# The other experts' rows added to x by accumulating gathers, and the last expert's second product made in two column halves

## The chip, the core and the metric

The kernel runs on one core of a Trainium2 chip. The core has a matrix engine (TensorE, PE in the rows), a vector engine (VectorE, DVE), a scalar engine (ScalarE, ACT), a general engine (GpSimd, POOL) and an engine that mostly issues transfers (SyncE, SP). Each engine works through its own instructions in order and they meet at semaphores; sixteen DMA engines move data between DRAM and the on-chip memory SBUF. The metric is device time in microseconds, the median of several executions. All arithmetic is float32.

## What is computed

The program is a two-layer network on 512 tokens of width 1024. The change touches only the end of the second layer, a mixture of eight experts of which each token takes two, and the normalisation behind it:

```python
def swiglu(x, w1, w3, w2):
    return (jax.nn.silu(x @ w1) * (x @ w3)) @ w2

def moe_ffn(x, router_w, router_b, w1, w3, w2):
    logits = (x @ router_w).astype(jnp.float32) + router_b
    top_val, top_idx = lax.top_k(logits, TOP_K)
    weights = jax.nn.softmax(top_val, axis=-1)
    combine = jnp.sum(jax.nn.one_hot(top_idx, N_EXPERTS, dtype=jnp.float32) * weights[..., None], axis=-2)
    y = jnp.zeros_like(x)
    for e in range(N_EXPERTS):
        y = y + combine[..., e:e + 1].astype(x.dtype) * swiglu(x, w1[e], w3[e], w2[e])
    return y

...
        x = layer_norm(DN_ALPHA * x + y, ln_g[layer, 1], ln_b[layer, 1])
    return x
```

Here D_MODEL is 1024, D_FF_EXPERT 1408, N_EXPERTS 8, TOP_K 2.

## The kernel before

Tokens are sorted to experts: each expert has 128 slots, and 32 more for an overflow, which a branch skips where an expert has no more than 128 tokens (`further`, line 1453). `moe` (line 1765) loops over the experts. For each it gathers its tokens' rows, turns them so that the contraction lies on the partitions, and makes the two products with w1 and w3 in three column chunks (`up`, line 1410; 512, 512 and 384 columns). `turn` (line 1469) turns the gated result, and `down` (line 1493) makes the product with w2. Every float32 product is made of three matmuls: a weight block is loaded by SP into one of nine raw buffers (`moe_raw`), ACT casts it to a rounded part (`whi`, line 1164), and DVE subtracts to get the rest (`wlo`, line 1165). A raw buffer is free again after the branch in which the overflow slots would use it. While `ring` is set four more buffers serve.

For experts 0 to 6 the product y of 128 slots by 1024 columns is copied from PSUM by ACT (columns 0 to 511) and DVE (512 to 1023) and written by POOL to a DRAM array Y (lines 1532 to 1534); the overflow slots follow one step later (`down_more`, line 1538). Each token then knows two rows of Y (`slot`, made in `slots`, line 1676); a token's place in the last expert points at a zero row. In the last expert `ask_rows` (line 1707) gathers these rows, a block of 128 tokens and one of its two choices at a time, into the former ring buffers, and `take_rows` (line 1714) scales them on ACT by the token's weight and adds them to x on POOL:

```python
self.nc.scalar.mul(rows, rows, self.wt[:, tb, j:j + 1])
for half in range(2):
    xs = self.x[tb][half]
    self.nc.gpsimd.tensor_add(xs, xs, rows[:, half * 512:(half + 1) * 512])
```

The last expert's own product does not go through Y. `last` (line 1739) splits it, spreads it over the tokens by one-hot matmuls (`ohl`, lines 1755 to 1758), adds it to x on DVE (line 1760) with the token's weight, takes statistics (`stats`, line 248), normalises (`layer_norm`, lines 255 to 267) and stores.

The instructions of each engine are put in order by a scheduler from the written order and from priorities: `high_priority` and `hot` pull what they enclose forward, and `chain` keeps the weight loads in order. `weights` (line 1656) turns the router's two best scores into weights per token and expert (`cw`).

## Time and profile before

| | |
|---|---|
| device time, median of 3 runs | 2099.56 us (2098.76 to 2100.62) |
| the profiled execution: time / span of its instructions | 2099.76 us / 2098.0 us |
| PE busy | 2005.5 us, 96% |
| DVE busy | 1365.4 us, 65% |
| ACT busy | 916.3 us, 44% |
| POOL busy | 155.1 us, 7% |
| mean granted TensorE clock | 0.988 |

The span runs from the first instruction to the last; times in rows count from its start. The second layer's experts take about the last quarter of it. In a row of an engine's timeline stand the start, the duration, the engine, the line of the code and the operation, what it writes and from what, its shape and how many were merged; in brackets stand the time for which the engine was idle before it and what it waited for. Matmul durations overlap, so the rate of matmuls is read from their starts.

### The profile page before, as it was taken

The page shows a single profiled execution, that of the slowest core. Times are in us where ns is not written, and L with a number is a line of the kernel's source. Part 1 is how long each engine was busy: PE and PEld are TensorE (multiplying, and loading weights), DVE is VectorE, ACT ScalarE, POOL GpSimd, SP SyncE. Part 2 cuts the span into 40 slices and gives each one's busy share as a digit, 9 for nine tenths or more (in the row PEclk, how much of TensorE's full clock was granted, in tenths as well). Part 3 has the DMA queues.
Part 4 walks back from the last instruction along what each step waited for, and adds up shares of the span by engine and source line. Part 5 has one row for each costly group of instructions (what it writes and reads, how often), then busy time and mean ns, then how long its engine had stood idle before and what let it go on. Part 6 is the DMA issues. An engine that isn't in the chain of part 4 may idle for free. (4 is left out here: it accounts for less than half of the span.)

```text
span 2098.0 us, 31138 instructions
## 1 busy us (share of the span) xinstructions
PE 2005.5 (96%) x11240; PEld 1561.3 (74%) x11240; DVE 1365.4 (65%) x2732; ACT 916.3 (44%) x1561; POOL 155.1 (7%) x211
## 2 busy tenths in 40 slices
PE   8999999999999999999999999999989999999984
PEld 7767778778888888888767678778877766677663
DVE  5776779844563333236676779843668877788778
ACT  3464543333232222113454543332326666677663
POOL 1020200000000000000001200000010000000043
PEclk9999999999999999999999999999999999999997
DMA  5231213243243334333221213223538988898872
GB/s 166 71 78 37 58 51 91 81 126 101 91 151 95 101 94 133 91 100 115 77 57 44 70 36 90 84 64 101 196 112 313 350 296 304 284 351 304 291 284 78
DMA packets 274976, 294.56 MB, mean 140 GB/s; under 512 B 23852, under 2 KB 203416, under 8 KB 274808
## 3 DMA queue, kind: packets, MB, share of 16 engines
q1 hardware_dynamic: 267736, 273.90, 40.3%
q0 software_dynamic: 7072, 18.49, 2.8%
q8 instruction: 97, 1.59, 0.3%
q14 instruction: 71, 0.58, 0.1%
HBM read 276.74 MB, written 15.60 MB: 139 GB/s over the span
## 5 line engine op out<-in xcount | busy, mean ns | idle before, releaser
L99 DVE TENSOR_TENSOR wlo<-wraw,whi 128x1024 fp32r<-128x1024 f32 (+1 forms) x218 | 265.4, 1218 | 361.3 <-ACT whi L98 357.4
L98 ACT CAST whi<-wraw 128x1024 fp32r<-128x1024 f32 (+1 forms) x218 | 228.1, 1047 | 622.1 <-PE ps_mm L112 375.7
L113 PE MATMUL ps_mm<-xh,wlo 128*128 128x512 f32 (+1 forms) x1288 | 492.8, 383 | 3.1 <-DVE wlo L99 3.1
L111 PE MATMUL ps_mm<-xh,whi 128*128 128x512 f32 (+1 forms) x1288 | 494.6, 385 | 0.5 <-ACT whi L98 0.4
L112 PE MATMUL ps_mm<-xl,whi 128*128 128x512 f32 (+1 forms) x1288 | 492.4, 383 | 0.2 <-DVE xl L233 0.2
L113 PEld LDWEIGHTS ps_mm<-xh,wlo 128*128 128x128 f32 x1288 | 243.5, 189 | 49.0 <-DVE wlo L99 3.4
L112 PEld LDWEIGHTS ps_mm<-xl,whi 128*128 128x128 f32 x1288 | 243.5, 189 | 45.4 <-issue 2.1
L111 PEld LDWEIGHTS ps_mm<-xh,whi 128*128 128x128 f32 x1288 | 243.2, 189 | 45.3 <-issue 1.9
L1165 DVE TENSOR_TENSOR wlo<-mwraw,whi 128x1024 fp32r<-128x1024 f32 (+1 forms) x98 | 124.1, 1281 | 18.0 <-ACT whi L1164 16.6
L1164 ACT CAST whi<-mwraw 128x1024 fp32r<-128x1024 f32 (+1 forms) x98 | 95.9, 1006 | 16.4 <-PE ps_t L1515 10.2
L472 ACT COPY bt_pt<-ps_t 128x512 f32<-128x512 f32 (+2 forms) x80 | 41.8, 523 | 87.2 <-PE ps_t L467 86.7
L1165 DVE TENSOR_TENSOR mwlo<-mwraw,mwhi 128x1024 fp32r<-128x1024 f32 (+1 forms) x62 | 71.8, 1174 | 6.6 <-ACT mwhi L1164 6.2
L451 ACT ACTIVATE bt_pt<-ps_s,mx 128x256 f32<-128x256 f32 (+3 forms) x128 | 61.9, 488 | 17.5 <-DVE mx L445 14.2
L260 POOL TENSOR_TENSOR rs<-rs,mhalf 128x1 f32<-128x1 f32 x16 | 13.8, 861 | 721.0 <-DVE rs L259 721.0
L442 DVE TENSOR_REDUCE mx<-ps_s 128x2 f32<-128x512 f32 (+3 forms) x80 | 48.5, 607 | 22.5 <-PE ps_s L406 21.8
L1164 ACT CAST mwhi<-mwraw 128x1024 fp32r<-128x1024 f32 (+1 forms) x62 | 61.0, 999 | 3.1 <-DMA mwraw<-in_exp_w_dram 2.0
L1126 DVE TENSOR_TENSOR bt_pt<-bt_pt,ps_mm 128x512 f32<-128x512 f32 x22 | 15.1, 688 | 69.9 <-PE ps_mm L113 62.5
L622 DVE MAX8 m<-bt_pt 128x8 f32<-128x256 f32 (+2 forms) x96 | 53.7, 560 | 2.6
L467 PE MATMUL ps_t<-ident,bt_pt 128*128 128x128 f32 x272 | 45.1, 281 | 8.5 <-DVE bt_pt L461 5.9
L1165 DVE TENSOR_TENSOR wlo<-ring,whi 128x1024 fp32r<-128x1024 f32 (+1 forms) x45 | 51.4, 1158 | 2.5 <-ACT whi L1164 2.4
L623 DVE MATCH_REPLACE8 bt_pt<-m,bt_pt 128x256 f32<-128x256 f32 (+2 forms) x96 | 52.1, 543 | 0.0
L111 PE MATMUL ps_mm<-bt_o,whi 128*128 128x512 f32 x128 | 50.9, 397 | 0.4 <-ACT bt_o L524 0.4
(710 smaller groups left out, 4116.4 us busy)
## 6 DMA issues: line engine op xcount, KB each, us to landing
mwraw<-in_exp_w_dram SPq DMA_DIRECT2D x124, 512.0 KB
wraw<-in_w_in_dram SPq DMA_DIRECT2D x106, 512.0 KB
wraw<-in_ffn_w_dram SPq DMA_DIRECT2D x66, 512.0 KB
ring<-in_exp_w_dram SPq DMA_DIRECT2D x60, 512.0 KB
wraw<-in_exp_w_dram SPq DMA_DIRECT2D x32, 512.0 KB
mwraw<-in_exp_w_dram SPq DMA_DIRECT2D x36, 384.0 KB
wraw<-in_w_branch_dram SPq DMA_DIRECT2D x20, 512.0 KB
wraw<-in_w_out_dram SPq DMA_DIRECT2D x16, 512.0 KB
```

The lines of the kernel that those rows point to most:

```text
L98: nc.scalar.copy(h, src)
L99: (low or nc.vector).tensor_sub(l, src, h.bitcast(F32))
L111: mm(ps, wh, xh, start=start, stop=False)
L112: mm(ps, wh, xl, start=False, stop=False)
L113: mm(ps, wl, xh, start=False, stop=stop)
L442: nc.vector.tensor_reduce(mx[:, 0:nh], s3, op=OP.max, axis=AX.X)
L451: nc.scalar.activation(p3[:, h], s3[:, h], AF.Exp, bias=nm[:, h:h + 1], scale=0.125, accum_out=mx[:, 4 + h:5 + h])
L467: return nc.tensor.transpose(pt[:, i * P:(i + 1) * P], p3[:, h, kb * P:(kb + 1) * P], self.ident)
L622: nc.vector.max(m8, sc[:, :nk])
L623: nc.vector.match_replace(sc[:, :nk], m8, sc[:, :nk], REPL)
L1164: self.chain("hi", lambda: nc.scalar.copy(hi[:, :n], src))
L1165: self.chain("lo", lambda: nc.vector.tensor_sub(lo[:, :n], src, hi[:, :n].bitcast(F32)))
```

## The change

Experts' rows are now scaled before they are written to Y. `slot_weights` writes the combined weights to DRAM, gathers for every slot the row of weights of its token, and keeps them in `ws`; the overflow slots' weights are brought to `wso` by small copies. The copies out of PSUM in `down` and `down_more` become multiplications by these weights. Y is split into two arrays of 512 columns. `ask_rows` issues sixteen indirect gathers that add into x as they land; the scalings on ACT and the additions on POOL (`take_rows`) are gone. The last expert's second product (`down_last`) goes through the first 512 columns of w2, hands them to `last`, and then does the other 512; `last` now does one half of the columns, and the normalisation comes with the second. The load of a w2 block is two 128-row blocks of 512 columns instead of one of 1024. `weights` is called in expert 0 instead of expert 1. One-hot tables fall from three to two.

```diff
@@ -1498,9 +1498,6 @@
         nc.vector.memset(po, 0.0)
         late = []
         for f0 in range(0, EB, 2):
-            if e == NE - 1 and f0 in (2, 6):
-                self.take_rows(f0 // 4 + 1)
-                self.ask_rows(f0 // 4 + 2)
             fs = range(f0, min(EB, f0 + 2))
             raws = []
             for f in fs:
@@ -1523,15 +1520,14 @@
                             mm(po[q:q + 32], gto[:, f], w[:, hf * 512:(hf + 1) * 512], start=f < 2, stop=f >= EB - 2,
                                skip_group_check=True)
                 late = []
-        if e == NE - 1:
-            self.take_rows(TB - 1)
-            return p0, p1, po
         y = self.rf.tile([P, D], F32, name="yr", tag="yr", bufs=2)
         yo = self.rf.tile([P, 512], F32, name="yo", tag="yo", bufs=1)
         with self.tc.high_priority():
-            nc.scalar.copy(y[:, 0:512], p0)
-            nc.vector.tensor_copy(y[:, 512:], p1)
-            nc.gpsimd.dma_start(self.Y[e * P:(e + 1) * P, :], y)
+            w = self.ws[:, e, e:e + 1]
+            nc.scalar.activation(y[:, 0:512], p0, AF.Copy, scale=w)
+            nc.vector.tensor_scalar(y[:, 512:], p1, w, None, op0=OP.mult)
+            for hf in range(2):
+                nc.gpsimd.dma_start(self.Y[hf][e * P:(e + 1) * P, :], y[:, hf * 512:(hf + 1) * 512])
             nc.scalar.copy(yo, po)
         return yo
 
@@ -1540,10 +1536,43 @@
         ps = self.ps("y")
         nc.tensor.matmul(ps[0:64], self.ident64, yo, start=True, stop=True)
         ys = self.rf.tile([64, 512], F32, name="ys", tag="ys", bufs=1)
-        nc.vector.tensor_copy(ys, ps[0:64])
+        nc.vector.tensor_scalar(ys, ps[0:64], self.wso[:, e:e + 1], None, op0=OP.mult)
         r = (NE - 1) * P + 32 * e
         for hf in range(2):
-            nc.gpsimd.dma_start(self.Y[r:r + 32, hf * 512:(hf + 1) * 512], ys[32 * hf:32 * hf + 32])
+            nc.gpsimd.dma_start(self.Y[hf][r:r + 32, :], ys[32 * hf:32 * hf + 32])
+
+    def down_last(self, gT, g, b):
+
+        nc, I, e = self.nc, self.I, NE - 1
+        mm = nc.tensor.matmul
+        gt, gto = gT
+        for half in range(2):
+            cs = slice(half * 512, half * 512 + 512)
+            ps, po = [self.ps(t) for t in (("s", "o"), ("t", "mm"))[half]]
+            nc.vector.memset(po, 0.0)
+            late = []
+            for f0 in range(0, EB, 2):
+                m = min(2, EB - f0)
+                raw = self.moe_raw()[:, :m * 512]
+                with self.tc.high_priority():
+                    self.chain("load", lambda: nc.sync.dma_start(
+                        raw.rearrange("p (k c) -> p k c", k=m),
+                        I["exp_w2"][0, e, f0 * P:(f0 + m) * P, cs].rearrange("(k p) c -> p k c", p=P)))
+                h, l = self.moe_split(raw)
+                for i in range(m):
+                    f = f0 + i
+                    wh, wl = h[:, i * 512:(i + 1) * 512], l[:, i * 512:(i + 1) * 512]
+                    self.chain("mm", lambda: mm(ps, gt[:, 0, f], wh, start=f == 0, stop=False))
+                    mm(ps, gt[:, 0, f], wl, start=False, stop=False)
+                    mm(ps, gt[:, 1, f], wh, start=False, stop=f == EB - 1)
+                    late.append((f, raw[:, i * 512:(i + 1) * 512]))
+                if len(late) >= 4 * HOLD or f0 + 2 >= EB:
+                    with self.further(e):
+                        for f, w in late:
+                            q = 32 * (f % 4)
+                            mm(po[q:q + 32], gto[:, f], w, start=f < 4, stop=f >= EB - 4, skip_group_check=True)
+                    late = []
+            self.last(half, ps, po, g, b)
 
     def rest(self, dp):
 
...
@@ -1671,7 +1700,22 @@
             nc.vector.tensor_scalar(cw[:, tb], self.oh[:, 0, tb], wt[:, tb, 0:1], None, op0=OP.mult)
             nc.vector.tensor_scalar(c1, self.oh[:, 1, tb], wt[:, tb, 1:2], None, op0=OP.mult)
             nc.vector.tensor_add(cw[:, tb], cw[:, tb], c1)
-        return wt, cw
+        return cw
+
+    def slot_weights(self, dp):
+
+        nc, mp = self.nc, self.rf
+        d = dp.tile([T, NE], F32, name="d_wt")
+        nc.gpsimd.dma_start(d.rearrange("(b p) e -> p b e", p=P), self.cw)
+        self.ws = mp.tile([P, 10, NE], F32, name="ws")
+        for c in (*range(NE - 1), 8, 9):
+            self.gather(d, self.tok[:, c:c + 1], "ws", self.ws[:, c])
+
+        self.wso = mp.tile([64, NE], F32, name="wso")
+        for e in range(NE - 1):
+            r = 32 * (e % 4)
+            for h in range(2):
+                nc.vector.tensor_copy(self.wso[32 * h:32 * h + 32, e:e + 1], self.ws[r:r + 32, 8 + e // 4, e:e + 1])
 
     def slots(self):
 
...
@@ -1702,71 +1746,61 @@
 
         z = mp.tile([P, D], F32, name="zero", tag="xg", bufs=2)
         nc.vector.memset(z[0:1], 0.0)
-        nc.gpsimd.dma_start(self.Y[(NE - 1) * NS:(NE - 1) * NS + 1, :], z[0:1])
-
-    def ask_rows(self, *tbs):
+        for hf in range(2):
+            nc.gpsimd.dma_start(self.Y[hf][(NE - 1) * NS:(NE - 1) * NS + 1, :], z[0:1, 0:512])
+
+    def ask_rows(self):
 
         self.ring = None
-        for tb in tbs:
-            for j in range(2):
-                self.gather(self.Y, self.slot[:, j, tb:tb + 1], "yg", self.yg[:, tb % 2 * 2 + j])
-
-    def take_rows(self, *tbs):
-        for tb in tbs:
-            for j in range(2):
-                rows = self.yg[:, tb % 2 * 2 + j]
-                self.nc.scalar.mul(rows, rows, self.wt[:, tb, j:j + 1])
-                for half in range(2):
-                    xs = self.x[tb][half]
-                    self.nc.gpsimd.tensor_add(xs, xs, rows[:, half * 512:(half + 1) * 512])
+        for j in range(2):
+            for tb in range(TB):
+                for hf in range(2):
+                    self.nc.gpsimd.indirect_dma_start(
+                        out=self.x[tb][hf], out_offset=None, in_=self.Y[hf], compute_op=OP.add,
+                        in_offset=bass.IndirectOffsetOnAxis(ap=self.slot[:, j, tb:tb + 1], axis=0))
 
     def last_begin(self):
 
         nc, mp = self.nc, self.rf
         num = self.num_t
-        ido = mp.tile([P, 2], F32, name="ido")
-        nc.vector.memset(ido, -1.0)
-        for h in range(2):
-            for i in range(2):
-                r = 32 * (2 * i + h)
-                nc.vector.tensor_copy(ido[r:r + 32, h:h + 1], self.own[96:128, 9:10])
+
+        ido = mp.tile([P, 1], F32, name="ido")
+        for i in range(4):
+            nc.vector.tensor_copy(ido[32 * i:32 * i + 32], self.own[96:128, 9:10])
         self.ohl = []
-        for n, col in enumerate((self.own[:, NE - 1:NE], ido[:, 0:1], ido[:, 1:2])):
+        for n, col in enumerate((self.own[:, NE - 1:NE], ido)):
             t = mp.tile([P, T], F32R, name="ohl", tag="g", bufs=3)
             nc.vector.tensor_scalar(t, num, col, None, op0=OP.is_equal)
             self.ohl.append(t)
 
-    def last(self, pss, g, b):
+    def last(self, half, ps, po, g, b):
 
         nc, mp = self.nc, self.rf
         mm = nc.tensor.matmul
         hl = []
-        for n, ps in enumerate(pss):
-            t = mp.tile([P, 2, 512], F32R, name="yl", tag="xg" if n == 2 else "yr", bufs=2)
-            nc.scalar.copy(t[:, 0], ps)
-            nc.vector.tensor_sub(t[:, 1], ps, t[:, 0].bitcast(F32))
+        for n, src in enumerate((ps, po)):
+            t = mp.tile([P, 2, 512], F32R, name="yl", tag=("yr", "xg")[n], bufs=2)
+            nc.scalar.copy(t[:, 0], src)
+            nc.vector.tensor_sub(t[:, 1], src, t[:, 0].bitcast(F32))
             hl.append(t)
-        tags = ("r", "y", "s", "t", "o", "mm", "mm", "mm")
         for tb in range(TB):
             ts = slice(tb * P, (tb + 1) * P)
-            for half in range(2):
-                ps = self.ps(tags[tb * 2 + half])
-                a, o = self.ohl[0][:, ts], self.ohl[1 + half][:, ts]
-                mm(ps, a, hl[half][:, 0], start=True, stop=False)
-                mm(ps, a, hl[half][:, 1], start=False, stop=False)
-                mm(ps, o, hl[2][:, 0], start=False, stop=False)
-                mm(ps, o, hl[2][:, 1], start=False, stop=True)
-                xs = self.x[tb][half]
-                nc.vector.scalar_tensor_tensor(xs, ps, self.cw[:, tb, NE - 1:NE], xs, op0=OP.mult, op1=OP.add)
-                self.stats(tb, half)
-            self.layer_norm(tb, g, b, spread=True)
-            self.store_x(tb, self.out)
+            out = self.ps((("r", "y", "mm", "mm"), ("r", "y", "s", "t"))[half][tb])
+            for n in range(2):
+                for i in range(2):
+                    mm(out, self.ohl[n][:, ts], hl[n][:, i], start=n == 0 and i == 0, stop=n == 1 and i == 1)
+            xs = self.x[tb][half]
+            nc.vector.scalar_tensor_tensor(xs, out, self.cw[:, tb, NE - 1:NE], xs, op0=OP.mult, op1=OP.add)
+            self.stats(tb, half)
+            if half:
+                self.layer_norm(tb, g, b, spread=True)
+                self.store_x(tb, self.out)
 
     def moe(self, dp):
 
         nc, I, mp = self.nc, self.I, self.rf
         self.xe = self.xp.tile([P, 2, 2, KB, P], F32R, name="xe", tag="xh")
-        self.ring = self.yg = self.xp.tile([P, 4, D], F32, name="ring", tag="xl")
+        self.ring = self.xp.tile([P, 4, D], F32, name="ring", tag="xl")
         with self.hot():
             last = self.count()
             with self.tc.issue_after(last.ins):
@@ -1802,22 +1836,22 @@
                     self.tokens(e + 2)
                     if e == 0:
                         self.dispatch(range(4, 8))
+                        self.cw = self.weights("")
+                        self.slot_weights(dp)
                     if e == 1:
-                        self.wt, self.cw = self.weights("")
                         self.slots()
                     if e == NE - 1:
-                        self.ask_rows(0)
+                        self.ask_rows()
                         g, b = self.ln_consts(1, 1)
             last = st
             if e + 1 < NE:
                 st = self.up(e + 1, 0)
             self.turn(last)
             if e == NE - 1:
-                self.take_rows(0)
-                self.ask_rows(1)
                 self.last_begin()
-            yo = self.down(e, gT)
-        self.last(yo, g, b)
+                self.down_last(gT, g, b)
+            else:
+                yo = self.down(e, gT)
 
 
 def build(tc, I, out, taps=None, stage=99):
@@ -1825,7 +1859,7 @@
         n = Net(tc, I, out, ctx, taps)
         dp = ctx.enter_context(tc.tile_pool(name="dp", bufs=1, space=bass.MemoryType.DRAM))
         n.xs = [dp.tile([T, D], F32, name=f"xs{i}") for i in range(3)]
-        n.Y = dp.tile([(NE - 1) * NS + 1, D], F32, name="Y")
+        n.Y = [dp.tile([(NE - 1) * NS + 1, 512], F32, name=f"Y{i}") for i in range(2)]
         n.dinv = [[dp.tile([16, 64, 64], F32, name=f"inv{i}{j}") for j in range(3)] for i in range(2)]
         n.xsrc = I["x"][0]
         n.load_x(n.xsrc)
```

The scheduler's order changes in three places that matter below. On DVE in expert 0, after the second chunk's accumulator is cleared (the split of the next weight block and the gating product follow):

```order
 L1436 UNCONDITIONAL_BRANCH x2
 L1416 MEMSET ps_mm 128x512
+L1718 COPY wso<-ws 32x1 x8
 L1165 TENSOR_TENSOR wlo<-mwraw,whi 128x1024
 L1448 TENSOR_TENSOR g<-g,ps_mm 128x512
```

Eight of the fourteen copies into `wso` now stand there; they need a gather into `ws`.

On POOL in the last expert, before, from the last write of Y on (`ring` receives the gathered rows, `bt_x` is x):

```order
L1546 DMA Y<-ys 32x512 x2
L1329 DMA ring<-Y,slot_i 128x1024 x2
L1436 REGISTER_ALU x2
L1436 COMPARE_AND_BRANCH
L1436 UNCONDITIONAL_BRANCH x2
L1329 DMA ring<-Y,slot_i 128x1024 x2
L1721 TENSOR_TENSOR bt_x<-bt_x,ring 128x512
```

and after, the last five gathers (`bt_x_12892` is the second half of x's second block, 12895 and 12896 the third block, 12899 and 12900 the fourth; all sixteen follow on the last write of Y, the first choice of all blocks before the second):

```order
L1758 DMA bt_x_12892<-Y1_190,slot_i_15628 128x512
L1758 DMA bt_x_12895<-Y0_189,slot_i_15628 128x512
L1758 DMA bt_x_12896<-Y1_190,slot_i_15628 128x512
L1758 DMA bt_x_12899<-Y0_189,slot_i_15628 128x512
L1436 REGISTER_ALU x2
L1436 COMPARE_AND_BRANCH
L1436 UNCONDITIONAL_BRANCH x2
L1758 DMA bt_x_12900<-Y1_190,slot_i_15628 128x512
```

POOL now has only transfers to issue there, and additions no longer stand between them.

On DVE at the end of the last expert, before (`yl` is the split product, the L1165 rows are the last weight splits):

```order
L1165 TENSOR_TENSOR wlo<-mwraw,whi 128x1024 x2
L1747 TENSOR_TENSOR yl<-ps_o,yl 128x512
L1747 TENSOR_TENSOR yl<-ps_s,yl 128x512
L1747 TENSOR_TENSOR yl<-ps_t,yl 128x512
L1760 SCALAR_TENSOR_TENSOR bt_x<-ps_r,cw,bt_x 128x512
L1760 SCALAR_TENSOR_TENSOR bt_x<-ps_y,cw,bt_x 128x512
L248 BN_STATS bst<-bt_x 128x6 x2
```

and after, where the first column half is added to x's four blocks (ps_r, ps_y, ps_mm, ps_mm) among and behind the last weight splits of the second half:

```order
L1793 SCALAR_TENSOR_TENSOR bt_x<-ps_r,cw,bt_x 128x512
L1165 TENSOR_TENSOR wlo<-mwraw,whi 128x1024 x2
L1165 TENSOR_TENSOR mwlo<-mwraw,mwhi 128x512
L248 BN_STATS bst<-bt_x 128x6
L1793 SCALAR_TENSOR_TENSOR bt_x<-ps_y,cw,bt_x 128x512
L1793 SCALAR_TENSOR_TENSOR bt_x<-ps_mm,cw,bt_x 128x512
L248 BN_STATS bst<-bt_x 128x6 x2
L1793 SCALAR_TENSOR_TENSOR bt_x<-ps_mm,cw,bt_x 128x512
L1552 MEMSET ps_mm 128x512
L248 BN_STATS bst<-bt_x 128x6
```

Behind these rows stand two branches and then the split of the second half's y. All four additions of the first half, and so the gathers of the first halves, come before it.

## Rows read from the trace of the kernel before

**Rows 1.** busy time by stretch, experts' stage: us, engines, granted clock, DMA share, GB/s:

```profile
core 0: us, PE busy (x) PEld busy (x) DVE busy (x) ACT busy (x) POOL busy (x), PEclk, DMA share, GB/s
...
1860.00:1920.00 60.00, 58.68 (x276) 44.29 (x275) 53.29 (x61) 44.42 (x58) 1.63 (x3) 1.00 0.93 331
```

**Rows 2.** PE in order of time, last expert; wait and releaser in brackets:

```profile
start us, us, engine line op out<-in xcount [idle before <-releaser]
...
2027.82 0.45 PE L1428 MATMUL ps_mm<-whi,xe 128*128 128x384 f32 x1 [1.59 <-ACT whi L1164]
2029.28 0.69 PE L1429 MATMUL ps_mm<-wlo,xe 128*128 128x384 f32 x1 [1.01 <-DVE wlo L1165]
...
2057.91 0.80 PE L1514 MATMUL ps_s<-wlo,gt 128*128 128x512 f32 x1 [7.01 <-DVE wlo L1165]
2058.50 0.63 PE L1515 MATMUL ps_s<-whi,gt 128*128 128x512 f32 x1
2058.93 0.63 PE L1514 MATMUL ps_t<-wlo,gt 128*128 128x512 f32 x1
...
2063.13 0.39 PE L1513 MATMUL ps_t<-mwhi,gt 128*128 128x512 f32 x1
2063.36 0.40 PE L1514 MATMUL ps_s<-mwlo,gt 128*128 128x512 f32 x1
```

**Rows 3.** ACT in order of time, last expert:

```profile
2025.90 1.15 ACT L1718 ACTIVATE ring<-ring,wt 128x1024 f32<-128x1024 f32 x1 [3.05 <-DMA ring<-Y,slot_i]
```

**Rows 4.** DVE in order of time, last expert:

```profile
2049.02 9.97 DVE L1165 TENSOR_TENSOR wlo<-mwraw,whi 128x1024 fp32r<-128x1024 f32 x2
2058.91 2.35 DVE L1165 TENSOR_TENSOR mwlo<-wraw,mwhi 128x1024 fp32r<-128x1024 f32 x2
```

**Rows 5.** POOL in order of time, last expert, and its gathers together (ns):

```profile
2018.45 2.38 POOL L1329 DMA_INDIRECT ring<-Y,slot_i  x1 [4.02 <-issue]
...
2049.39 7.38 POOL L1721 TENSOR_TENSOR bt_x<-bt_x,ring 128x512 f32<-128x512 f32 x6
...
L1329 POOL DMA_INDIRECT ring<-Y,slot_i x8: 938/1612/2377, 2018.5 to 2047.7; - x8
```

**Rows 6.** the end: ACT, then DVE in order of time:

```profile
2070.01 0.59 ACT L1746 CAST yl<-ps_s 128x512 fp32r<-128x512 f32 x1 [2.74 <-PE ps_s L1515]
...
2072.70 0.75 DVE L1760 SCALAR_TENSOR_TENSOR bt_x<-ps_r,cw,bt_x 128x512 f32<-128x512 f32 x1 [0.78 <-PE ps_r L1758]
...
2074.05 1.28 DVE L248 BATCH_NORM_STATS2 bst<-bt_x 128x6 f32<-128x512 f32 x2
```

**Rows 7.** DMA queues and landings, 2016 to 2052 us:

```profile
q1 hardware_dynamic: 3634, 8.72, 62.4%
q0 software_dynamic: 1198, 4.29, 31.0%
...
DMA to landing us min/median/max: 5.1/7.9/9.5
```

**Rows 8.** first expert: DVE, POOL, PE in order of time, then DMA landings:

```profile
1576.49 0.16 DVE L1673 TENSOR_TENSOR cw<-cw,cw 128x8 f32<-128x8 f32 x1
...
1583.96 1.23 DVE L1165 TENSOR_TENSOR wlo<-mwraw,whi 128x1024 fp32r<-128x1024 f32 x1 [2.32 <-ACT whi L1164]
...
1617.36 0.31 DVE L1732 COPY ido<-own 32x1 f32<-32x1 f32 x2
...
1572.69 0.97 POOL L1329 DMA_INDIRECT xg<-xs,tok  x1 [0.72 <-ACT mwhi L1164]
1573.96 0.94 POOL L1329 DMA_INDIRECT xg<-xs,tok  x1 [0.30 <-issue]
...
1585.24 0.49 PE L1429 MATMUL ps_t<-wlo,xe 128*128 128x512 f32 x1 [0.20 <-DVE wlo L1165]
...
Y<-ys POOLq DMA_DIRECT2D x4, 64.0 KB, 4.7
...
Y<-zero POOLq DMA_DIRECT2D x1, 4.0 KB, 1.8
```

2 lines of the change are left out of this document (1 added, 1 removed).

## The prediction

> **What bounds the kernel now.** I read the per-stretch table first. Through the experts' stage TensorE (PE) is busy about 98 to 99 per cent of the time at full granted clock [rows 1], so anything that makes PE wait there is paid in full. That stops being true in the last expert, where I read PE's own timeline for its idle gaps: from 2025.9 to 2070 us it waits eight times, 14.8 us in all; three of them stand in the rows, with 9.6 us [rows 2], the other five are 0.2 to 2.8 each. Each gap names its releaser. The first is ScalarE (ACT), which stood 3.05 us before the row scaling of line 1718 because the gathered rows had not landed [rows 3]; a weight's split stood behind it. The long ones are VectorE (DVE), and there the split that normally takes 1.2 us took 9.97 us for two [rows 4], exactly while GpSimd (POOL) ran six of its additions into x (line 1721) without a pause [rows 5]. So the last expert is held up by the very work that adds the other experts' rows to x. Behind each long gap PE also runs at the lower of its two levels (1.2 against 2.4 GHz): matmuls stand 0.43 us apart instead of 0.23 [rows 2].
>
> **What goes.** With the additions on POOL and the scalings on ACT gone, I take out the gaps and the slow stretches. Gaps: 14.8 us. Slow clock: 9 matmuls of 384 columns after 2029.3 at 0.32 instead of 0.17 us (1.35 us), 3 or 4 of 512 columns after 2049.15 and 12 after 2057.9 at 0.43 instead of 0.23 us (3.0 us). Together 19.2 us. The last product ends at 2070.0 (the cast that waits for it starts at 2070.01 [rows 6]), so without waits it would end at 2050.8.
>
> **What moves into the product.** Half of the final one-hot matmuls (16 of 32) now run after the first half of the columns, inside the product: 16 x 0.23 = 3.7 us on PE, and one more branch (about 0.3 us). PE alone would then be done at 2054.8. The number of product matmuls, weight bytes and splits is the same as before; the weights merely come as two sets of half-width columns. The first half's additions and statistics stand on DVE behind nearly all splits of the second half (order, third piece), so they are hidden.
>
> **What the end loses.** From the end of the product to the end of the span there are 28.0 us, mostly DVE in order: addition, statistics, normalisation [rows 6]. Of eight additions (two take 1.35 us, start to start, 0.67 each) and eight statistics (0.60 us) four of each are now done earlier: 5.1 us. The tail becomes 22.9 us.
>
> **The gathers.** Eight gathers of 512 KB become sixteen of 256 KB that add into x. They wait, as before, for the last write of Y, so they start at 2018.5 at the earliest [rows 5]. POOL's time per gather was 0.94 to 2.38 us, in the middle 1.6 [rows 5], with 0.3 between: the sixteenth is issued at 2018.5 + 15 x 1.9 = 2047. No row shows an adding transfer, so I bound it. From 2016 to 2052 the DMA engines were almost full: the weights' queue took 62.4 per cent of 36 us for 8.72 MB, the gathers' queue 31.0 per cent for 4.29 MB [rows 7]. At the plain price all of it lands near 2052, as before, and the last weights soon enough: the product ends at about 2055. If each gather costs double, because x has to be read too, 11.2 us more of engine time is wanted (31 per cent of 36), everything lands at 2061 and the last weights at about 2058, since the two queues share; with a split and three matmuls behind it (2.5 us) the product ends at 2060.5. A gain over the plain price is excluded, as the same bytes arrive. I take the middle, 2057.5. First what the rows show: plain gathers cost per byte the same engine time as plain loads (7.2 per cent per MB in both queues). The Trainium skill's page "Collectives: The Full Stack" (Part 3, the bandwidth ceiling) says that an adding transfer reads two sources through one read ring and so runs at half the rate of a copy. By that page the sum would be the upper end, 2060.5; no row here shows it.
>
> **What is added in the first expert.** The weights per slot are written to DRAM, gathered by nine small transfers, and copied by DVE into a small tile. Order shows the eight copies on DVE right after the clearing of the accumulator and ahead of a split and of the gating product (first piece). DVE is in order, so if the gathers have not landed it stands, and PE behind it. I follow the chain. The combined weights are ready at 1576.65 [rows 8]. POOL is free by then; its write is issued at about 1577 and lands 1.8 us later at best (the zero row) and 4.7 us at worst (ys), I take 3.5: 1580.5. Five gathers must be issued before the one that the copies wait for has gone: consecutive gathers started 1.27 us apart, so the fifth starts at 1585.6. Its landing costs between 1.8 us (a small write) and 4.3 (the fastest 512 KB gather); I take 2.8, nearer the small one, since it moves 4 KB: 1588.4. Eight copies at 0.155 each [rows 8] add up to 1.2. DVE reaches its next split at 1589.5, before at 1583.96. That split feeds a matmul that PE wanted at 1585 already (it waited 0.20 us for it), so PE stands 5.5 us more. Behind such a gap the clock is low for a while; the slow stretch after the first gaps of the last expert cost 1.35 us, so about 1.4. Sum 6.9 us, in bounds of 1 us (fast landings, 0.94 us pitch) to 10.5 us (slow landings, 1.5 us pitch). Nothing gives this back: PE is full from there to 2018, and all later times shift by it. The second group of copies (six) stands behind the copies that ran at 1617.36 [rows 8]; its gather can be asked for as soon as the second dispatch's tokens are there, before these copies. I count no wait, and at most 1 us, within the bounds. Scaling while y leaves PSUM replaces a copy of the same shape on ACT and on DVE: nothing. Two writes per expert instead of one cost POOL 0.6 us each in seven places, while it idles.
>
> **Sum.** Product end 2057.5 + tail 22.9 + first expert 6.9 = 2087.3 of span, against 2098.0. The profiled execution took 2099.76, that is 1.8 beyond its span; its time lies 0.2 above the median of the runs, which I neglect. Forecast 2089.1, a gain of 0.5 per cent.
>
> **Rivals.** (a) Adding costs double: 2060.5 + 22.9 + 6.9 + 1.8 = 2092.1. For it: x is read as well. Against: only the read side doubles. (b) The first expert does not stand: the gathers land before DVE arrives. For it: DVE waited 2.32 us there anyway [rows 8]. Against: five issues alone fill that. Time 2089.1 - 5.9 (the lower bound of 1 us) = 2083. (c) The gathers become the bound. On DVE the addition into the fourth block of x, first half, stands ahead of the second half's split of y (order, third piece), so that block's second gather, the fifteenth and last but one on POOL (order, second piece), holds the whole tail: addition, clearing, statistics, two splits (some 3.7 us), and then what follows the first addition, 25.3 us before and 20.2 without the 5.1: the end comes 24 us after its landing. At POOL's longest issue (2.38 + 0.3) the fifteenth starts at 2018.5 + 14 x 2.68 = 2056, lands 9.5 us later (the slowest landing) at 2065.5, and the time is 2065.5 + 24 + 6.9 + 1.8 = 2098: no change. The rows show POOL's issue at 0.94 and 0.97 us in the first expert [rows 8] and at 1.61 in the middle in the last [rows 5]. [...] (d) Slower: the same mechanism, with more than 3.5 us per gather. The point is the landing of the fifteenth at 2099.8 - 24 - 6.9 - 1.8 = 2067; at 4.2 us per gather it lands at 2081 and the time is 2114. For it: every second gather adds to a block that the first must have finished, and 16 are half as large. Against: eight are issued in between, so landings overlap. (e) DVE's slow splits had another cause than POOL: the 9.97 us remain, 2098. Against: the overlap in the rows.
>
> **How the numbers follow.** Forecast (one to two times the plain price, with the wait in the first expert) 0.45; (a) in full 0.20; (b) 0.10; (c) 0.13; (d) 0.09; (e) 0.03. Measurement tells about 0.2 per cent, 4.2 us: faster means below 2095.4. Forecast, (a) and (b) are faster, and a third of (c): 0.79. The rest of (c), and (e): 0.12. (d): 0.09. The range from 2079 (plain price, short wait) to 2099 leaves out (d) and some of both ends, together 2 in 10.
>
> **What would show it.** Right: no gap on PE from 2026 on above 1 us but for weights; splits at 1.2 us to the end; a gap of some 5 us on PE at 1585 with DVE's small copies as releaser; DMA landings of the gathers; a tail of 22.9 us. Wrong: PE waiting for weights in the second half (then adding costs more than double), DVE standing before the fourth block's addition (then (c) or (d)), or no gap at 1585 (b).

## The result: slower, by 0.7 per cent

| kernel | median, us | runs | ratio to the kernel before, 95% interval |
|---|---|---|---|
| before | 2100.09 | 2098.76 to 2101.74 | |
| changed | 2115.66 | 2112.02 to 2117.80 | 1.0071 [1.0057, 1.0086] |

The forecast was 2089.1 us, with 0.09 for slower. The profiled execution of the changed kernel took 2114.69 us, with a span of 2112.8 (2098.0 before).

To see where the 14.8 us of span arose I cut it at two marks that every kernel below has: the first gather of the experts' stage on POOL (`ring<-xs,tok`), and the first matmul of the last expert's last column chunk (line 1428 of before, 384 columns). Stretch 1 is from mark to mark, stretch 2 from the second mark to the end of the span (us):

| | first mark | second mark | span | stretch 1 | stretch 2 |
|---|---|---|---|---|---|
| before | 1570.70 | 2023.08 | 2098.0 | 452.4 | 74.9 |
| changed | 1572.35 | 2037.44 | 2112.8 | 465.1 | 75.4 |

1.6 us are there before the stage begins, in code that the change does not touch (over the experiments below the first mark lies anywhere from 1568.2 to 1572.3); 12.7 us are lost between the marks; and the rest of the last expert, for which I had expected a gain, takes 0.5 us more than before.

### The profile page after: what moved, and what is told of

It is laid out like the page before. It is cut to its first block, busy times and chain, and to the rows that moved or that the text cites. A ratio compares the mean times of both kernels' runs of the same rounds, so it can differ in the third digit from the quotient of the medians.

```text
span 2112.8 us, 31186 instructions
## 1 busy us (share of the span) xinstructions
PE 2015.6 (95%) x11240; PEld 1566.5 (74%) x11240; DVE 1356.1 (64%) x2747; ACT 909.8 (43%) x1555; POOL 162.2 (8%) x221
## 5 line engine op out<-in xcount | busy, mean ns | idle before, releaser
L1165 DVE TENSOR_TENSOR wlo<-mwraw,whi 128x1024 fp32r<-128x1024 f32 (+2 forms) x98 | 112.3, 1158 | 18.7 <-ACT whi L1164 17.5
L1164 ACT CAST whi<-mwraw 128x1024 fp32r<-128x1024 f32 (+2 forms) x98 | 95.7, 1000 | 15.7 <-DMA mwraw<-in_exp_w_dram 14.9
L1165 DVE TENSOR_TENSOR mwlo<-mwraw,mwhi 128x1024 fp32r<-128x1024 f32 (+2 forms) x63 | 71.7, 1148 | 9.1 <-ACT mwhi L1164 8.6
L451 ACT ACTIVATE bt_pt<-ps_s,mx 128x256 f32<-128x256 f32 (+3 forms) x128 | 61.8, 487 | 17.8 <-DVE mx L445 14.4
L1164 ACT CAST mwhi<-mwraw 128x1024 fp32r<-128x1024 f32 (+2 forms) x63 | 61.4, 990 | 8.0 <-DMA mwraw<-in_exp_w_dram 7.7
L1165 DVE TENSOR_TENSOR wlo<-ring,whi 128x1024 fp32r<-128x1024 f32 (+1 forms) x45 | 51.7, 1161 | 3.7 <-ACT whi L1164 3.6
```

The costliest lines, as they stand in the source:

```text
L451: nc.scalar.activation(p3[:, h], s3[:, h], AF.Exp, bias=nm[:, h:h + 1], scale=0.125, accum_out=mx[:, 4 + h:5 + h])
L1164: self.chain("hi", lambda: nc.scalar.copy(hi[:, :n], src))
L1165: self.chain("lo", lambda: nc.vector.tensor_sub(lo[:, :n], src, hi[:, :n].bitcast(F32)))
```

## The profile after

**First expert.** The answers to [rows 8]. DVE in order of time (start, duration, line, operation; in brackets the idle time and what ended it):

```profile
1582.80 0.48 DVE L1416 MEMSET ps_mm<- 128x512 f32 x1
1594.31 1.24 DVE L1718 COPY wso<-ws 32x1 f32<-32x1 f32 x8 [11.02 <-DMA ws<-d_wt,tok]
1595.57 1.23 DVE L1165 TENSOR_TENSOR wlo<-mwraw,whi 128x1024 fp32r<-128x1024 f32 x1
```

POOL there: the write of the weights, then the first and the fifth of the five small gathers that are issued in a row:

```profile
1578.74 0.85 POOL L1709 DMA_DIRECT2D d_wt<-cw  x1 [2.21 <-DVE slot_f L1743]
1583.82 0.98 POOL L1329 DMA_INDIRECT ws<-d_wt,tok  x1 [4.23 <-DMA d_wt<-cw]
...
1588.86 0.94 POOL L1329 DMA_INDIRECT ws<-d_wt,tok  x1 [0.30 <-issue]
```

DVE stood 11.02 us in front of eight tiny copies. The write landed 5.1 us after its issue (1578.74 to 1583.82), the fifth gather 5.4 us after its own (1588.86 to 1594.3). The split behind the copies feeds PE, whose rows show the price, and below them the last expert, as the answer to [rows 2]:

```profile
1596.86 0.79 PE L1429 MATMUL ps_t<-wlo,xe 128*128 128x512 f32 x1 [10.01 <-DVE wlo L1165]
...
1599.22 0.63 PE L1429 MATMUL ps_t<-wlo,xe 128*128 128x512 f32 x1
...
2045.79 0.44 PE L1428 MATMUL ps_mm<-whi,xe 128*128 128x384 f32 x1 [1.86 <-ACT whi L1164]
...
2066.96 0.63 PE L1565 MATMUL ps_s<-whi,gt 128*128 128x512 f32 x1
2067.39 0.63 PE L1566 MATMUL ps_s<-wlo,gt 128*128 128x512 f32 x1
...
2074.09 0.50 PE L1565 MATMUL ps_t<-mwhi,gt 128*128 128x512 f32 x1 [2.64 <-ACT mwhi L1164]
...
2076.90 0.63 PE L1791 MATMUL ps_y<-yl,ohl 128*128 128x512 f32 x1
...
2080.72 1.56 PE L1791 MATMUL ps_mm<-yl,ohl 128*128 128x512 f32 x6
...
2088.17 0.40 PE L1567 MATMUL ps_t<-mwhi,gt 128*128 128x512 f32 x1
```

PE's 0.20 us of [rows 8] became 10.01, and matmuls behind it stood 0.43 us apart (duration 0.63), the lower clock level; the granted clock from 1590 to 1610 is 0.74, against 1.00 before. In the last expert the gap of 7.01 us is gone; eleven small gaps of 0.3 to 2.6 us stand in its place, released by ACT and DVE, and from 2058.9 to 2069 PE runs at the lower level again. The L1791 rows are the first half's one-hot matmuls, among the second half's product (ps_t).

**What the last expert waits for.** ACT in order of time, in place of [rows 3] and the first of [rows 6]:

```profile
2066.97 1.04 ACT L1164 CAST whi<-mwraw 128x1024 fp32r<-128x1024 f32 x1 [2.82 <-DMA mwraw<-in_exp_w_dram]
...
2073.00 1.04 ACT L1164 CAST mwhi<-wraw 128x1024 fp32r<-128x1024 f32 x1 [2.94 <-DMA wraw<-in_exp_w_dram]
...
2079.70 0.62 ACT L1164 CAST mwhi<-mwraw 128x512 fp32r<-128x512 f32 x1
2088.60 0.58 ACT L1783 CAST yl<-ps_t 128x512 fp32r<-128x512 f32 x1 [8.28 <-PE ps_t L1567]
```

ACT casts a weight as soon as it lands and then stands for the next: the weights come late. The last is cast at 2079.70, and yet the product ends only at 2088.2: when the last weight is cast, PE still has some 8 us of work in its queue. Stretches of the last expert (busy time of each engine, granted clock, DMA share, GB/s):

```profile
core 0: us, PE busy (x) PEld busy (x) DVE busy (x) ACT busy (x) POOL busy (x), PEclk, DMA share, GB/s
...
2040.00:2050.00 10.00, 6.83 (x34) 5.97 (x33) 5.64 (x9) 3.73 (x7) 8.77 (x5) 0.92 1.09 265
2050.00:2060.00 10.00, 7.45 (x26) 4.84 (x25) 3.39 (x5) 3.42 (x5) 8.18 (x6) 0.84 1.10 264
2060.00:2070.00 10.00, 8.11 (x17) 4.38 (x17) 4.71 (x6) 4.03 (x7) 4.24 (x3) 0.55 1.10 263
```

The DMA engines are full (share 1.1) but move only 264 GB/s; in the kernel before they moved 412 from 2028 to 2048. The 16 gathers on POOL (ns, lowest, median and highest), with their landing, answer to [rows 5] and [rows 7]; below them DVE, a pair of splits and the tail, to [rows 4] and [rows 6]:

```profile
L1758 POOL DMA_INDIRECT bt_x<-Y,slot_i x16: 1544/1544/2745, 2033.2 to 2063.3; - x16
...
DMA to landing us min/median/max: 8.3/9.6/10.9
```

```profile
2080.22 0.75 DVE L1793 SCALAR_TENSOR_TENSOR bt_x<-ps_r,cw,bt_x 128x512 f32<-128x512 f32 x1 [1.45 <-PE ps_r L1791]
2080.89 2.35 DVE L1165 TENSOR_TENSOR wlo<-mwraw,whi 128x1024 fp32r<-128x1024 f32 x2
...
2097.67 1.98 DVE L266 TENSOR_TENSOR bt_x<-bt_x,bt_lc 128x512 f32<-128x512 f32 x2
```

With no additions on POOL and no scalings on ACT the splits take 1.2 us each to the end, as foreseen. The first half's addition on DVE waited for PE, not for a gather. The tail, from the cast at 2088.60, is 24.2 us (28.0 before).

## The experiments

Two theories at the start. For the place of the loss: the wait in the first expert is paid in full (A), or made up later (B). For the last expert: adding makes the gathers dear for the DMA (A1), or the halved rows do (B1, B2).

**1. The copies moved behind expert 0's last split**, from `slot_weights` to `down_more`.

```diff
-        for e in range(NE - 1):
...
-                nc.vector.tensor_copy(self.wso[...], self.ws[...])
+        if e == 0:
+            with self.tc.issue_after(self.links["lo"].ins):
+                for i in range(NE - 1):
...
+                        nc.vector.tensor_copy(self.wso[...], self.ws[...])
```

> The changed kernel with one thing moved: the 14 small copies that fill the other rows' weights (wso<-ws, on DVE) stand behind expert 0's last split instead of in the middle of its second third. The nine small gathers and everything else stay. Theory A (the loss sits at expert 0: DVE waited 11.02 us there for the fifth of the nine gathers, the splits behind it came late and PE stood 10.01 us and then ran at half clock): the changed kernel had fallen 12.7 us further behind the kernel before between the start of the mixture of experts and the last expert; without the wait most of that comes back, 10 to 13 us, so 2103 to 2106 us, about 1.002 of the kernel before. Theory B (expert 0's wait is made up later by loads that run ahead, and the last expert, held by its transfers, sets the end): no more than 4 us come back, 2111 to 2116.

Measured: 2106.46 us (2105.15 to 2108.76), ratio 1.0037 [1.0023, 1.0050]; 9.2 us come back, a little less than the 10 to 13 of theory A. In the first expert PE's gap is gone (0.3 us). In its place comes a side effect: with the copies moved, DVE's order at expert 1 is another, and there PE stands for DVE's clearing of an accumulator (line 1416), while DVE itself stands 5.6 us for ACT in front of its next clearing (line 1498); PE's rows:

```profile
1665.43 1.51 PE L1441 MATMUL ps_mm<-mwraw,xo 128*32 128x384 f32 x8 [2.46 <-DVE ps_mm L1416]
1666.71 2.79 PE L1441 MATMUL ps_mm<-ring,xo 128*32 128x384 f32 x16
```

The granted clock was 0.91 from 1660 to 1700, 1.00 in the kernel before. Stretch 1 is 457.6 us: 5 us more than before in place of 12.7.

**2. The kernel before with the slot weights alone.**

```diff
                         self.dispatch(range(4, 8))
+                        self.wt, self.cw = self.weights("")
+                        self.slot_weights(dp)
                     if e == 1:
-                        self.wt, self.cw = self.weights("")
```

> The kernel before with one part of the change alone: the slot weights are made at expert 0 (one store of the weights, nine small gathers, 14 copies on DVE at the place of the changed kernel), and nobody uses them. Theory A: DVE stands there as in the changed kernel, and PE with it, so the kernel is 11 to 13 us slower than the kernel before, 2111 to 2113 us. Theory B: the wait is made up later, within 4 us of the kernel before, 2100 to 2104. If DVE's wait needs the rest of the change (the doubled stores of Y, the moved loads), it isn't there at all and the time is that of before.

Measured: 2113.66 us (2111.71 to 2113.80), ratio 1.0065 [1.0052, 1.0078], 13.7 us more than the kernel before (2099.93 in these runs). The edit also moves the call of `weights` to expert 0; the eighth run, which keeps that move and loses the wait, shows that it costs nothing. The two waits, from 1560 to 1660 us (total, times, longest):

```profile
DVE wso L1689 <- DMA ws<-d_wt,tok: 10.3, 1, 10.3
...
PE ps_t L1429 <- DVE wlo L1165: 7.9, 1, 7.9
```

Theory A holds: this small part of the change costs nearly the whole of the difference, and nothing behind it gives the time back. (Stretch 1 is 12.0 us longer than before.)

**3. Plain gathers, over x.**

```diff
-                        out=self.x[tb][hf], out_offset=None, in_=self.Y[hf], compute_op=OP.add,
+                        out=self.x[tb][hf], out_offset=None, in_=self.Y[hf],
```

> The changed kernel with the 16 big gathers plain: they write the gathered rows over x instead of adding to it (x is left out of the sum), in the same order, size and place. Theory A1 (adding makes a gather cost the DMA engines about twice as much: the queue took 4.95 us for a MB against 2.6 in the kernel before, the whole DMA moved 264 GB/s against 415, and the last expert's weights came late): the last expert's product ends 5 to 10 us earlier against its start, the DMA moves over 380 GB/s in the stretch of the gathers, time 2105 to 2110. Theory B1 (the price comes from the halved rows of 2 KB, 16 gathers instead of 8, and the weights' halved rows, not from adding): within 2 us of the changed kernel, 2113 to 2118, and the DMA's rate in the stretch stays near 264 GB/s.

Measured: 2099.24 us (2096.89 to 2102.91), ratio 1.0000 [0.9991, 1.0008]: 16.4 us less than the changed kernel, with every instruction at its place (the gathered rows overwrite x, so x is left out of the sum). More than theory A1 expected. Stretch 2 fell from 75.4 to 62.0. The two DMA queues, 2040 to 2060 us (packets, MB, share of 16 engines), in this kernel:

```profile
q1 hardware_dynamic: 2353, 4.52, 59.3%
q0 software_dynamic: 1065, 3.49, 44.3%
```

and in the changed kernel:

```profile
q0 software_dynamic: 1334, 2.44, 66.5%
q1 hardware_dynamic: 1599, 2.84, 42.7%
```

Queue 0 holds the gathers, queue 1 the weights. Worked out from the rows: 44.3% of 20 us for 3.49 MB is 2.54 us of the engines for a MB, 66.5% for 2.44 MB is 5.45. A MB added took 2.15 times the engine time of a MB gathered plainly. The adding gathers also came in smaller packets (2.44 MB in 1334, 1.8 KB each, against 3.3 KB), so how much of the 2.15 is the addition and how much the packets is not separated.

**4. No gathers at all.**

```diff
     def ask_rows(self):
...
-        for j in range(2):
...
-                    self.nc.gpsimd.indirect_dma_start(
```

> The changed kernel with the 16 big gathers left out (the other experts' rows don't reach x). It gives the floor of the last expert. Theory A1: the weights come without waits, the last expert's product goes at PE's pace, 2.05 us for a step and about 15 to 19 us less than in the kernel before from its start to its end, where the changed kernel had it 3.9 us more: 2096 to 2102 in all, with expert 0's wait still in it. Theory B2 (the weights come late because of the halved second product, whose loads have rows of 2 KB): the waits for weights stay, 2108 to 2116.

Measured: 2093.96 us (2092.63 to 2095.07), ratio 0.9972 [0.9962, 0.9983], stretch 2 is 54.9. Theory A1, and 2 us below its range: without gathers PE waits for no weight in the last expert (its waits from 2022 us on are 1.0 us in all, none for a weight). Set against the third run, even plain gathers cost 5.3 us.

**5. The halves undone.**

```diff
-                self.last_begin()
-                self.down_last(gT, g, b)
-            else:
-                yo = self.down(e, gT)
+                self.last_begin()
+            yo = self.down(e, gT)
+        self.last(yo, g, b)
```

(with `last_begin` and `last` of the kernel before)

> The changed kernel with its last expert's second product undone: whole rows of 1024 columns, one long accumulation, and the end of the kernel before behind it; slot weights and adding gathers stay. Theory A (the halves are worth what the tail showed, 28.0 us before and 24.4 after, and nothing in the product): about 3.6 us slower than the changed kernel, 2118 to 2121. Theory B (the halves cost something themselves, since each load then fetches rows of 2 KB in place of 4 KB while the DMA is short): the product ends earlier and makes up for the tail, 2110 to 2116.

Measured: 2105.78 us (2103.68 to 2108.70), ratio 1.0029 [1.0017, 1.0040]. Neither expectation: the halves cost the changed kernel 9.9 us, more than theory B's range allows. Stretch 2 is 68.9. The two queues, 2040 to 2060 us:

```profile
q0 software_dynamic: 1099, 2.00, 54.2%
q1 hardware_dynamic: 1127, 4.01, 53.5%
```

The weights get 4.01 MB in 20 us where they got 2.84, and the packets of the two queues go about one for one, here as there. From this came a new theory, tested in the eleventh run.

**6. The halves with DVE adding the rows** (on the kernel before).

```diff
-                self.nc.scalar.mul(rows, rows, self.wt[:, tb, j:j + 1])
-                for half in range(2):
...
-                    self.nc.gpsimd.tensor_add(xs, xs, rows[:, half * 512:(half + 1) * 512])
+                self.nc.vector.scalar_tensor_tensor(xs, self.yg(tb, j)[:, half * 512:(half + 1) * 512],
+                                                    self.wt[:, tb, j:j + 1], xs, op0=OP.mult, op1=OP.add)
```

(with the changed kernel's `down_last` and `last`)

> The kernel before with the halves of the last second product, and the gathered rows taken by DVE: eight plain gathers of whole rows into two spare buffers, and 16 instructions on DVE, x = rows * weight + x, in place of 8 scalings on ACT and 16 adds on POOL. No slot weights, no adding gathers, so neither of the two prices found so far (13.7 us from the second run, 16.4 us from the third against the changed kernel). Theory A (the two prices are all that was wrong with the change): 2099.2 of the third run less 13.7 is 2085.5; 16 of these on DVE at about 0.7 us are 11.2 us, of which a part lies in front of the end: 2086 to 2093, 0.3 to 0.7% faster than the kernel before. Theory B (DVE becomes the bound in place of POOL, its splits stand behind adds that wait for gathers): 2097 to 2104.

Measured: 2097.80 us (2093.74 to 2099.91), ratio 0.9987 [0.9979, 0.9996]. Theory B: stretch 2 is 73.7, almost that of before. The additions stand on DVE ahead of the first half's split of y, and PE's one-hot matmuls wait for that (PE, 2022 to 2095 us):

```profile
PE ps_r L1791 <- DVE yl L1784: 7.0, 2, 4.1
```

**7. Half of the adding gathers.** In `ask_rows`:

```diff
-        for j in range(2):
+        for j in range(1):
```

> The changed kernel with 8 of the 16 adding gathers (the first choice of every token; the second choice's rows don't reach x). With none the time was 2094.0, with all 2115.7. Theory A (each adding gather takes its share of the DMA from the weights, one after the other): half way, 2102 to 2107. Theory C (the first gathers are hidden by loads that ran ahead and only the last ones reach the end): 2094 to 2099. The other way round, above 2109, it would be the first ones that hold the weights and the later ones are hidden.

Measured: 2102.92 us (2100.37 to 2105.09), ratio 1.0012 [1.0003, 1.0021]. Between none (2094.0) and all (2115.7) half way is 2104.8; theory A. The first eight cost 9.0 us, the second eight 12.7.

**8. The copies without what they wait for.**

```diff
-                nc.vector.tensor_copy(self.wso[...], self.ws[r:r + 32, 8 + e // 4, e:e + 1])
+                nc.vector.tensor_copy(self.wso[...], self.cw[r:r + 32, e // 4, e:e + 1])
```

> The changed kernel with the 14 small copies reading a tile that is there long before (the tokens' weights in place of the gathered ones, so the rows past the 128th of an expert get wrong weights); the nine small gathers stay. DVE doesn't wait at expert 0. Theory A (the wait costs what the second run paid for it, 13.7 us, and the first run got only 9.2 back because its moved copies brought DVE's work at expert 1 into another order, PE stood there 2.5 us and ran at half clock): 2102 to 2104. Theory B (the wait itself is worth 9 us, and what is left of the 13.7 is the price of the nine gathers and the store): 2105 to 2108.

Measured: 2102.70 us (2099.04 to 2104.28), ratio 1.0015 [1.0006, 1.0024], 13.0 us less than the changed kernel; stretch 1 is 453.0, within 0.6 us of before. Theory A: the wait alone is the price; the nine gathers and the write cost nothing that shows.

**9. Whole columns, and the copies on POOL.** The fifth run's kernel, all of it computed:

```diff
-                nc.vector.tensor_copy(self.wso[32 * h:32 * h + 32, e:e + 1], self.ws[r:r + 32, 8 + e // 4, e:e + 1])
+                nc.gpsimd.tensor_copy(self.wso[32 * h:32 * h + 32, e:e + 1], self.ws[r:r + 32, 8 + e // 4, e:e + 1])
```

> The fifth run's kernel (whole columns, slot weights, 16 adding gathers) with its 14 small copies on POOL, where nobody waits behind them, in place of DVE. Everything is computed. Theory A (the wait at expert 0 is a price by itself, 13.0 us from the eighth run, and adds to what the whole columns gave back, 9.9 us): 2105.8 less 13.0 is 2092.8; 2090 to 2096, 0.3% under the kernel before. Theory B (without the wait the last expert only waits longer for its transfers): 2099 to 2105.

Measured: 2095.31 us (2092.91 to 2100.14), ratio 0.9980 [0.9971, 0.9990]; 2092.8 was expected, 2095.3 lies inside theory A's bounds: 10.5 of the 13.0 us come back. POOL now stands for the gathers, for 4.54 us, and nobody behind it does:

```profile
1595.25 4.20 POOL L1687 COPY wso<-ws 32x1 f32<-32x1 f32 x8 [4.54 <-DMA ws<-d_wt,tok]
```

This kernel is 20.4 us faster than the changed one and 0.2 per cent faster than the kernel before. (Its profiled execution, 2100.14 us, is the longest of its eleven runs, so its stretch 2, 72.6, tells little.)

**10. Whole columns, DVE adding the rows** (on the kernel before; a pair of additions behind eight of the eleven splits).

```diff
+                for tb, j in TAKE.get(f, ()) if e == NE - 1 else ():
+                    with self.tc.high_priority(), self.tc.issue_after(self.links["lo"].ins):
+                        self.take_rows(tb, j)
+                    if (tb, j) == (0, 1):
+                        self.ask_rows(3)
```

(and `take_rows` as in the sixth run)

> The kernel before with one thing changed, the way in which the rows reach x: eight plain gathers, six of them asked for at once (the free half of the first product's input is a third pair of buffers), and 16 instructions x = rows * weight + x on DVE, one behind each split of the last second product, in place of 8 scalings on ACT and 16 adds on POOL. Whole columns, no slot weights, no adding gathers. From the start of the last expert's last third to the end of the span it took 74.9 us before, 68.9 in the fifth run. Theory A (POOL's adds, which slowed DVE's splits to up to 10 us, were the cost; plain gathers leave the weights their share): 60 to 66 us, 2084 to 2091 in all. Theory B (the sixth run's fault comes back, splits queue behind adds on DVE, 0.74 us each): 72 us or more, 2096 to 2102.

Measured: 2097.16 us (2093.09 to 2099.56), ratio 0.9989 [0.9980, 0.9998]. Theory B by the time; stretch 2 is 71.5 us, just under its 72. The views by stretch show DVE at its limit:

```profile
2040.00:2050.00 10.00, 6.05 (x22) 3.78 (x22) 10.00 (x12) 7.64 (x9) 3.36 (x2) 0.96 0.92 358
2050.00:2060.00 10.00, 5.23 (x14) 3.27 (x13) 10.00 (x14) 1.11 (x2) 0.00 (x0) 0.67 0.10 41
```

and PE waits for splits (2015 to 2075 us): 

```profile
PE ps_s L1519 <- DVE mwlo L1168: 5.6, 3, 4.7
PE ps_s L1519 <- DVE wlo L1168: 3.2, 2, 2.6
```

DVE, without a pause from 2040 to 2060, had the second product's splits and the additions to do at once.

**11. The packets alone.** The fifth run's kernel, each weight of the last second product fetched in two transfers:

```diff
-                    self.chain("load", lambda: nc.sync.dma_start(raw, I["exp_w2"][0, e, f * P:(f + 1) * P, :]))
+                        for cs in (slice(0, 512), slice(512, 1024)):
+                            self.chain("load", lambda: nc.sync.dma_start(
+                                raw[:, cs], I["exp_w2"][0, e, f * P:(f + 1) * P, cs]))
```

> The fifth run's kernel (whole columns, adding gathers) with each weight of the last second product fetched by two transfers of 512 columns, rows of 2 KB in place of 4 KB; the same bytes, the same matmuls. In the 20 us in which both queues were full the weights got 4.01 MB with rows of 4 KB (fifth run) and 2.84 MB with rows of 2 KB (the changed kernel), with 1127 and 1599 packets against 1099 and 1334 of the gathers. Theory D (the DMA serves the two queues about packet for packet, so weights in smaller packets get less of it beside adding gathers): the weights get under 3.2 MB in 20 us and the time goes up to 2109 to 2116. Theory E (the order of the halves' matmuls was what cost 10 us, not the packets): 2104 to 2108, with about 4 MB in 20 us.

Measured: 2112.54 us (2111.45 to 2116.24), ratio 1.0064 [1.0049, 1.0080], 6.8 us more than the fifth run with the same bytes and matmuls. The queues, 2040 to 2060 us:

```profile
q0 software_dynamic: 1436, 2.62, 70.7%
q1 hardware_dynamic: 1462, 2.58, 39.4%
```

Theory D: again one packet for one, so rows of half the size bring the weights 2.58 MB in place of 4.01 beside the adding gathers. Of the halves' 9.9 us I put 6.8 down to the packets and the other 3.1 to the order on PE below; neither share is isolated fully, as this run also issues twice as many loads, and the 3.1 has no run of its own. The third run sets a limit to theory D: beside plain gathers the weights got 2353 packets to 1065, so one for one is shown only beside adding gathers.

**12. Whole columns without gathers.** The fifth run's kernel with the fourth run's edit.

> The fifth run's kernel (whole columns) with the 16 adding gathers left out (the other experts' rows don't reach x), to be set against the fourth run (halves, no gathers, 2094.0 us): with nothing beside the weights on the DMA, what are the halves worth by themselves? Theory A (their gain is the tail's, 28.0 us before and 24.4 after, and comes in full when the weights aren't held): 3 to 5 us slower than the fourth run, 2097 to 2099. Theory B (rows of 2 KB cost about as much as the tail gives even alone, 385 to 395 GB/s against 410): within 1.5 us of the fourth run. From this also follows what the 16 adding gathers cost with rows of 4 KB beside them, from the fifth run's 2105.8.

Measured: 2092.82 us (2089.38 to 2094.03), ratio 0.9964 [0.9950, 0.9977]. Theory B's result, though not by its reason, since PE waits for no weight in either kernel: the halves are worth nothing even alone. The casts behind the product's end, on ACT, in this kernel:

```profile
2059.57 0.59 ACT L1748 CAST yl<-ps_s 128x512 fp32r<-128x512 f32 x1 [2.04 <-PE ps_s L1512]
```

and in the fourth run's, with halves:

```profile
2067.11 0.58 ACT L1777 CAST yl<-ps_t 128x512 fp32r<-128x512 f32 x1 [7.67 <-PE ps_t L1567]
```

From the second mark (2032.93 and 2036.48) to the cast it is 26.6 us with whole columns and 30.6 with halves; from the cast to the end of the span 28.1 and 24.3. The 4.0 us of work moved forward lengthen the product by what they take off the tail.

**The account.** The medians of four of these kernels make a path in four steps from the kernel before to the changed one. The second step is several edits at once, and the kernel before had medians from 2099.7 to 2100.7 beside the different runs, so a step is good to about 1 us:

| step | us |
|---|---|
| before (median beside these runs) | 2099.9 |
| slot weights, DVE waits for them (run 2) | +13.7 = 2113.7 |
| gathers, scalings and POOL's additions out (run 12) | -20.8 = 2092.8 |
| 16 adding gathers beside rows of 4 KB (run 5) | +13.0 = 2105.8 |
| the halves: rows of 2 KB, and PE's order (changed) | +9.9 = 2115.7 |

## Why the prediction was wrong, point by point

**What goes: right.** I took out 19.2 us of gaps and slow clock. Without gathers and additions the product of run 12 lasts 26.6 us from the second mark, in the kernel before 46.9: 20.3 us less. With the additions on POOL and the scalings on ACT gone the splits took 1.2 us in the changed kernel, so rival (e) is out; which of the two held them no run separates, the overlap in [rows 4] and [rows 5] points to POOL.

**What moves into the product: right in size** (4.0 us), by runs 4 and 12.

**What the end loses: mis-sized**, 3.8 us instead of 5.1. The four additions and statistics did move, but DVE's instructions of the normalisation stretched while POOL worked on its share of it (line 267 from 2097.23, 1.27 us): 1.98 us for a pair at 2097.67 where 1.28 is usual. Forecast and measurement leave a net gain of 1.1 and about none: the halves had nothing to offer that could pay for their packets.

**The gathers: the term that failed most.** I took 2.7 us (2057.5 against 2054.8), with bounds from 0.2 to 5.7. Measured are 13.0 us beside whole rows and 21.7 beside halves (2115.7 less 2094.0). The price of adding came out just above the bounds: twice the plain price was the upper end, 2.15 the measurement. The Trainium skill's page "Collectives: The Full Stack" (Part 3) has the adding phase of a collective at half the rate of the copying one, and the trace's 2.15 is close to that. What failed is the step from engine time to the weights' landing. "The two queues share" had the last weights land at 2058; less the 14.4 us by which the second mark moved, they were cast at 2065.3. I had left out that beside adding gathers the queues share by packets, that the change halves the weights' packets (2.84 MB in 20 us, 4.01 with whole rows), and that the weights' own price rises with it (3.0 us a MB, 2.7 with whole rows). And I let 2.5 us of work follow the last weight; from its cast to the product's end it was 8.9. PE had stood until 2074.09 for the second half's first weight; then the second half's casts followed within 6.7 us (2073.00 to 2079.70), while PE had 33 matmuls of the product and the first half's 16 one-hot ones in its queue, 11.3 us at 0.23 us each, and ran a part of them at the lower level (granted clock 0.50 from 2076 to 2078, 0.71 to 2080). PE's wait for weights in the second half is the first of the signs that I had named for being wrong. In the fifth run the granted clock stayed at 1.00 from 2040 to 2080.

**What is added in the first expert: the mechanism right, the size not.** Forecast 6.9 us, bounds to 10.5; measured 13.0 and 13.7. The write landed in 5.1 us (3.5 taken, 4.7 the worst I allowed), the gather in 5.4 (2.8 taken, 4.3 the worst): both above my bounds. How the time divides between the two varies: in the second run's profile the write landed in 2.5 us and the gather in 7.2. From the write's issue to the gather's landing it was 15.6 us here, 14.8 there, 11.4 in my sum; that stretch is the step that failed. I had sized the gather by its 4 KB, nearer to a small write from an idle moment; the DMA was at 0.93 of its time there (1570 to 1590), and at 0.76 in the 20 us after. The fifth gather and its pitch (1.25 us for 1.27) were right. PE's gap became 10.0 us, not 5.7, and the clock behind it cost about 3 us, not 1.4. That no later time gives it back was right.

**The rivals.** (b) did not occur: PE's gap at the first expert is there. (c) and (d), the fifteenth gather holding DVE, did not either: POOL started one every 2.0 us on average, the median issue took 1.54 us (1.61 before), and the fifteenth, issued at 2061.39, had landed by 2072.3 at the slowest landing, 14 us ahead of DVE's addition into its block at 2086.86. That (d)'s 2114 is near the result is chance, and its sum leaves out the landing that (c) counts. (a) named the right resource, with the same error of size. The sum was low by 6 to 7 us at the first expert and by some 19 at the gathers, and 79 in 100 for faster was far too sure: an unknown transfer was priced by engine time alone, without who else stands in the queues.

## What to carry to other kernels

Before moving an addition into a transfer, look at the DMA share of that stretch. Where it was full here, each MB added cost the engines what two plain ones do, and the load beside it got less the smaller its packets were, so keep its rows long. A tiny copy on an engine whose order feeds the matrix engine must not depend on a write and a gather just issued; put it on an engine where nobody stands behind it (run 9, which with whole columns is 0.2 per cent faster than the kernel before). And splitting a product to shorten the tail only moved work here (runs 4 and 12), as PE had no room for it earlier.

## What the hardware showed that I had not expected

- A write of 16 KB and a gather of 4 KB took 5.1 and 5.4 us to land while the weights filled the DMA, about what a gather of 512 KB took at best in the kernel before [rows 7]. In the second run's profile they took 2.5 and 7.2.
- With both queues full, adding gathers in one and weights in the other, the weights got 1.0 to 1.2 packets for one of the gathers (1127 to 1099, 1462 to 1436, 1599 to 1334), with rows of 4 KB and of 2 KB alike; beside plain gathers they got 2353 to 1065.
- Adding gathers took 5.45 us of the engines for a MB, plain ones 2.54.
- 32 by 1 copies took 0.155 us each on DVE and 0.52 on POOL (8 in 4.20).
